# Summing the squares of four query columns in plain float32 instead of two rounded parts

## Chip, cores and metric

The kernel runs on one core of a Trainium2 chip (trn2). The metric is the device time of one execution in microseconds (us). The kernel before was timed three times: 1103.29, 1103.33 and 1104.15 us, median 1103.33.

## The reference

One encoder block of hidden width 2048 on 272 tokens (16 learned meta tokens and 256 tokens of a 4 x 64 grid), all in float32. In outline:

```python
hn = rmsnorm(h, mix_norm_g[l])
proj = hn @ w_in[l]
q_a = rmsnorm(q_a.reshape(B, L, NA_HEADS, NA_HEAD_DIM), na_q_g[l])      # group A: 8 heads of 128
k_a = rmsnorm(k_a.reshape(B, L, NA_HEADS, NA_HEAD_DIM), na_k_g[l])
out_a = neighbourhood_attention(q_a, k_a, v_a, na_rpb[l], na_meta_bias[l])
out_b = mla_attention(cq, ckv, k_pe, ...)                               # group B: 8 heads, q and k of 192
h = h + jnp.concatenate([rmsnorm(out_a, na_out_g[l]), rmsnorm(out_b, mla_out_g[l])], -1) @ w_out[l]
h = h + conv_glu(rmsnorm(h, ffn_norm_g[l]), w_gate[l], w_up[l], conv_w[l], conv_b[l], w_down[l])
return h[:, N_META:]
```

What matters here is the rmsnorm of the queries of every head: for each token and head the squares over the head's 128 (group A) or 192 (group B) dimensions are summed, and the queries' scores are scaled by the reciprocal root of their mean plus eps.

## The kernel before

Tokens lie along the free axis and features along the 128 partitions. Token order is reversed, so the 256 grid tokens come first, and then the meta tokens. The convolution at the end still reaches one meta token, so queries are computed for 258 columns (`NT`): two blocks of 128 columns and **two meta queries**, columns 256 and 257. Heads are worked on in four pairs (`na_pair`, `mla_pair`), each pair once for group A and once for group B; with two heads that makes four small query columns per pair and group, the "few meta queries" of the change.

Precision: nearly every matmul is done three times on values split in two parts. `hi` is the value rounded to the type F32R, `lo` the remainder (`split_plain`: ScalarE copies into `hi`, VectorE subtracts into `lo`), and hi x hi, hi x lo and lo x hi are added up in a PSUM bank. A matmul whose operands have the type F32 is a plain float32 matmul; `ones_sum` (line 931) issues one with the constant `ones`.

The 128 main query rows of each block get their sum of squares on ScalarE, from transposed queries with an accumulating Square. The four small query columns get it from a matmul: `na_queries` (line 1310) and `mla_queries` (line 1497) let ScalarE write the squares into a small tile `sq8` (4 columns for group A, 8 for group B, whose second four are the rotary part). Then `small_sums` (line 1248) runs, once per pair and group, eight times in all: VectorE copies the squares, rounded, into the first half of `sq8r` (line 1251); GpSimd subtracts to get the remainder in the second half (line 1252); and TensorE multiplies each part with the rounded ones (`ones_r`), two matmuls of 128 x 4 by 128 x 2 for group A, four for group B, 24 in all. The sums go into `v`, `rstd` (line 923: logarithm, exponential, one refinement) turns them into the scale `rq`, and the heads' score tiles `na_tile` and `mla_tile` start after that.

Keys have a function of their own, `keys` (line 1161), 16 calls: squares of 272 columns, split into `hi` and `lo`, two matmuls with `ones_r` on the left, then `rstd` and a scaled, split key.

The order of the work is not that of the source. Every helper is a Python generator that yields the engine and an estimated cost before it issues its instruction (`ACT` line 247, `TT` line 253, `COPY` line 265, `PTT` on GpSimd line 277, `MM` line 287 with the costs of `cost` in line 281). A planner, `Flow` (line 124), keeps a clock per engine and always issues the instruction that could start earliest; on a hop between engines it adds 700 ns on the way to TensorE, 200 ns away from it and 140 ns otherwise (line 129). Each engine then executes its own instructions in exactly that order, and semaphores hold an instruction back until its inputs are there. So the costs decide the order, and a planned time that is too early makes an engine stand still in front of an instruction, with all that is queued behind it. `fl.cur.t += x` inside a helper moves its next instruction x ns later in the plan.

Slots (`Slots`, line 109) are sets of buffers that helpers take and give back in planned order. The sums, the score tiles and the attention outputs share two PSUM banks, `sps` (line 316). TensorE's main thread is `attention_weights` (line 1798): it goes through the projections pair by pair, and its matmuls (`mm3`, lines 734 to 736: two with the weights' `hi`, one with the weights' `lo`) fill TensorE between those of the attention. Weights arrive through SyncE's DMA queue and are split by ScalarE (`whi`) and VectorE (`wlo`). After the four pairs come the output projection (group B's heads `ob`, then group A's `oa`) and the gated MLP, whose up and down projections partly use a scheme of seven products.

Of the kernel before, what the change touches and what calls it, by code (L numbers as in the profile page):

```python
# [9 lines left out]
F32 = mybir.dt.float32  # L10
F32R = mybir.dt.float32r
AF = mybir.ActivationFunctionType
ALU = mybir.AluOpType
AX = mybir.AxisListType

P = 128
D_MODEL = 2048
SEQ = 256
# [200 lines left out]
def encoder_block(ctx: ExitStack, tc: tile.TileContext, io):  # L219
    nc = tc.nc  # L220
    ctx.enter_context(tc.manual_schedule())
    fl = Flow()
# [6 lines left out]
    apool = actx.enter_context(tc.tile_pool(name="apool", bufs=1))  # L229

    def tiles(pool, n, shape, name, dt=F32):
        return [pool.tile(shape, dt, tag=f"{name}{i}", name=f"{name}{i}") for i in range(n)]


    def size(ap):
        n = 1
        for s in ap.shape[1:]:
            n *= s
        return n
# [25 lines left out]
    def COPY(out, a):  # L265
        yield "dve", 68 + 1.04 * size(out)
        nc.vector.tensor_copy(out, a)
# [9 lines left out]
    def PTT(out, a, b, op):  # L277
        yield "pool", 90 + (2.7 if fl.cur.t < 4e5 else 3.9) * size(out)
        nc.gpsimd.tensor_tensor(out, a, b, op)  # L279

    def cost(l, r):
        n, m = size(r), l.shape[-1]
        if r.dtype != F32R:
            return max(1.69 * n, 3.33 * m, 50)
        return 0.445 * n + 3 if n >= 256 else max(0.84 * n, 0.84 * m, 27)

    def MM(items):

        yield "pe", sum(cost(l, r) for _, l, r, _, _ in items)
        for o, l, r, start, stop in items:  # L290
            nc.tensor.matmul(o, l, r, start=start, stop=stop)  # L291
# [18 lines left out]
    def one(slots):  # L310
        (t,) = yield slots, 1
        return t
# [169 lines left out]
    for w, f in enumerate(QUADS):  # L482

        g, end = f // 2, (*QUADS, MID)[w + 1] // 2
# [4 lines left out]
        for i in range(KC // 2):  # L489
            r = RowPair(io["w_up_s"][w][i], i, PW // 4, "up")  # L490
# [45 lines left out]
    n = len(others) - BEHIND  # L536
# [216 lines left out]
    ones = const("ones")  # L753
# [21 lines left out]
    for g in range(0, FC // 2 if MID_SUMS else 0, MID_SUMS or 1):  # L775
        n = min(MID_SUMS, FC // 2 - g)
        t = dpool.tile([P, n, PW // 4], F32, name=f"early_m{g}")
        w = io["w_down_m"][g : g + n].rearrange("g p c -> p g c")
        q, ev = PW // 4, Event()
        early.append((t, w[:, :, :q], w[:, :, 2 * q : 3 * q], ev))  # L780
        early_mid += [(t[:, i], ev) for i in range(n)]
    for g in range(FC // 2):
        ev, q, w = Event(), PW // 2, io["w_down_s"][g]
        if g % THIRD:
            t = dpool.tile([P, q], F32, name=f"early{g}")
            early.append((t, w[:, q : 2 * q], w[:, 2 * q : 3 * q], ev))
        else:
            t = dpool.tile([P, PW], F32, name=f"early{g}")
# [78 lines left out]
    p = pieces[0]  # L867
# [98 lines left out]
    ones_r = apool.tile([P, P], F32R, name="ones_r")  # L966
# [162 lines left out]
    qss = tiles(apool, 2, [P, 5 * QS + 4], "qs", F32R)  # L1129

    sq8 = tiles(apool, 2, [P, 8], "sq8")
    sq8r = tiles(apool, 2, [P, 2, 8], "sq8r", F32R)
    for t in [t.bitcast(F32) for t in qss] + sq8:
        nc.gpsimd.memset(t, 0.0)
    qss, sq8 = Slots(qss), Slots(list(zip(sq8, sq8r)))
    q_raw = Slots(tiles(apool, 1, [P, 3, NT], "qraw"))
    cols = tiles(apool, 8, [P, 8], "cols")
    for t in cols:
# [8 lines left out]
    for h in range(HEADS):  # L1147
        t = apool.tile([P, 2, NT], F32R, name=f"ob{h}")
        ob.append((t[:, 0, :], t[:, 1, :]))
        t = apool.tile([P, 2, NT], F32R, name=f"oa{h}") if h < 6 else hl[KC - HEADS + h]  # L1150
# [10 lines left out]
    def keys(ps, k, gain, n_dims, extra, ev):  # L1161

        hi, lo = k[:, 0, :], k[:, 1, :]
        kg = yield from one(scr)
        yield from ACT(kg[:, :L], ps[:, :L], AF.Copy)
        fl.put(acc, ps)
        sq, a, r = yield scr, 3
        v = sq[:, :L]
        yield from ACT(hi, kg[:, :L], AF.Square)
        yield from ACT(v, kg[:, :L], AF.Square)  # L1170
        yield from TT(lo, v, hi.bitcast(F32), ALU.subtract)
        yield ev_ones
        ss = yield from one(sps)
        yield from MM([(ss[:, :L], ones_r, hi, True, False), (ss[:, :L], ones_r, lo, False, True)])
        yield ev
        yield from STT(v, ss[:, :L], 1.0 / n_dims, extra, ALU.mult, ALU.add)
        fl.put(sps, ss)
        yield from rstd(r[:, :L], v, a[:, :L])
        fl.put(scr, a)
        fl.put(scr, sq)  # L1180
        yield ev_gains
        yield from STT(kg[:, :L], kg[:, :L], gain, r[:, :L], ALU.mult, ALU.mult)
        yield from split_plain(hi, lo, kg[:, :L])
        fl.put(scr, kg)
        return r
# [61 lines left out]

    def small_sums(q8, n):

        f, r = q8  # L1250
        yield from COPY(r[:, 0, : 4 * n], f[:, : 4 * n])
        yield from PTT(
            r[:, 1, : 4 * n], f[:, : 4 * n], r[:, 0, : 4 * n].bitcast(F32), ALU.subtract
        )
        yield ev_ones
        ss = yield from one(sps)
        m = [(g, i) for g in range(n) for i in range(2)]
        yield from MM(
            [(ss[:4, 0:2], r[:, i, 4 * g : 4 * g + 4], ones_r[:, 0:2], (g, i) == m[0], (g, i) == m[-1])
             for g, i in m]  # L1260
        )
        fl.put(sq8, q8)
        return ss
# [46 lines left out]
    def na_queries(s, pss):  # L1310
        q = yield from one(q_raw)
        s.q = yield from one(na_q)
        for c, ps in enumerate(pss):
            yield from ACT(q[:, c, :], ps[:, :NT], AF.Copy)
            fl.put(acc, ps)
        for c in range(2):
            fl.spawn(split_query(s, c, q))
        s.qs = yield from one(qss)
        fl.spawn(small_queries(s))
        w = yield from one(cols)  # L1320
        q8 = yield from one(sq8)
        yield from ACT(
            q8[0][:, 0:4].rearrange("p (c t) -> p c t", c=2), q[:, 0:2, SEQ:], AF.Square
        )
        pt = yield from one(tps)
        yield from TR(
            [(pt[:, (2 * c + i) * P : (2 * c + i + 1) * P], q[:, c, i * P : (i + 1) * P])
             for c in range(2) for i in range(2)]
        )
        fl.spawn(free_raw(s, q))  # L1330
        for j in range(4):
            t = pt[:, j * P : (j + 1) * P]
            yield from ACT(t, t, AF.Square, accum_out=w[:, j : j + 1])
        fl.put(tps, pt)
        ss = yield from small_sums(q8, 1)
        v = yield from one(v6)
        yield ev_em1c
        yield from STT(v[:, 0:4], w[:, 0:4], 1.0 / HD, em1_c, ALU.mult, ALU.add)
        yield from STT(v[:4, 4:5], ss[:4, 0:1], 1.0 / HD, em1_s, ALU.mult, ALU.add)
        fl.put(sps, ss)  # L1340
        s.rq = yield from one(rq6)
        yield from rstd(s.rq, v, w[:, 0:6])
        fl.put(v6, v)
        fl.put(cols, w)
        fl.set(s.ev_q)
# [151 lines left out]
    def mla_queries(s, pss):  # L1497
        q = yield from one(q_raw)
        s.q = yield from one(mq)
        for c in range(3):  # L1500
            yield from ACT(q[:, c, :], pss[c][:, :NT], AF.Copy)
            if c < 2:
                fl.put(acc, pss[c])
                fl.spawn(split_query(s, c, q))
        g, t, tmp = yield scr, 3
        yield from ACT(g[:, :NT], pss[2][:, :NT], AF.Copy, scale=gains[:, 2:3])
        fl.put(acc, pss[2])
        s.qs = yield from one(qss)
        fl.spawn(small_queries(s))
        fl.spawn(mla_rope(s, g, t, tmp))  # L1510
        w = yield from one(cols)
        q8 = yield from one(sq8)
        f = q8[0].rearrange("p (g c t) -> p g c t", g=2, c=2)
        yield from ACT(f[:, 0], q[:, 0:2, SEQ:], AF.Square)
        for c in range(2):
            e = slice(64 * c, 64 * c + 64)
            yield from ACT(f[e, 1, c, :], q[e, 2, SEQ:], AF.Square)
        for i in range(2):
            pt = yield from one(tps)
            sl = slice(i * P, (i + 1) * P)  # L1520
            yield from TR(
                [(pt[:, :P], q[:, 0, sl]), (pt[:, P : 2 * P], q[:, 2, sl]),
                 (pt[:, 2 * P : 3 * P], q[:, 1, sl])]
            )
            if i:
                fl.spawn(free_raw(s, q))
            for c in range(2):
                t = pt[:, c * QK_DIM : (c + 1) * QK_DIM]
                yield from ACT(t, t, AF.Square, accum_out=w[:, 2 * c + i : 2 * c + i + 1])
            fl.put(tps, pt)  # L1530
        ss = yield from small_sums(q8, 2)
        v = yield from one(v6)
        yield ev_emc
        yield from STT(v[:, 0:4], w[:, 0:4], 1.0 / QK_DIM, emc_c, ALU.mult, ALU.add)
        yield from STT(v[:4, 4:5], ss[:4, 0:1], 1.0 / QK_DIM, emc_s, ALU.mult, ALU.add)
        fl.put(sps, ss)
        s.rq = yield from one(rq6)
        yield from rstd(s.rq, v, w[:, 0:6])
        fl.put(v6, v)
        fl.put(cols, w)  # L1540
        fl.set(s.ev_q)
# [938 lines left out]
```

## Time and profile before

| what | value |
|---|---|
| median of three runs | 1103.33 us |
| the profiled execution's own time | 1103.1 us |
| its span, first to last instruction | 1101.3 us |
| granted TensorE clock | 0.999 |
| TensorE matmuls, busy | 1094.4 us, 8164 records |
| VectorE, busy | 1015.2 us, 1922 instructions |
| ScalarE, busy | 753.8 us, 1514 instructions |
| GpSimd, busy | 147.6 us, 217 instructions |
| DMA | 262.73 MB, mean 239 GB/s |

Times in the trace count from the first instruction. A matmul's record lasts from its start to the modelled arrival of its last result, so neighbouring matmuls overlap in the records and the distance from start to start tells how long TensorE was taken. Names of tiles stand without their numbers: `sq8` is printed as `sq`, `sq8r` as `sq8r`, the PSUM banks as `bank`.

### The profile page before, as it was taken

How to read it: one execution, taken by the hardware profiler on the slowest of the kernel's cores; microseconds unless marked ns; L12 is line 12 of the kernel's file. 1: busy time of each engine (PE TensorE's matmuls, PEld its weight loads, DVE VectorE, ACT ScalarE, POOL GpSimd, SP SyncE). 2: the span in 40 equal slices, each digit the busy share in tenths (PEclk: the TensorE clock that was granted, in tenths of full speed). 3: DMA queues.
4: the chain of work that ended last, by engine and by line, in shares of the span. 5: the costliest groups of instructions: out<-in, count | busy, mean ns of one | idle time of the engine just before them, and what ended most of it. 6: DMA issues, size and time to landing. Idle time of an engine off the chain costs nothing. (4 is left out here: it accounts for less than half of the span.)

```text
span 1101.3 us, 22419 instructions
## 1 busy us (share of the span) xinstructions
PE 1094.4 (99%) x8164; PEld 1046.1 (95%) x8164; DVE 1015.2 (92%) x1922; ACT 753.8 (68%) x1514; POOL 147.6 (13%) x217
## 2 busy tenths in 40 slices
PE   9999999999999999999999999999999999999998
PEld 9999999999999999999999999999999999888887
DVE  8969888888878989999999999999999989999997
ACT  8788979788646776666666666665665656666663
POOL 3211222323433400000000000000000000301041
PEclk9999999999999999999999999999999999999999
DMA  8775678577877778665766667767888879699891
GB/s 322 252 236 168 196 224 238 156 200 182 263 202 214 234 245 326 209 200 189 237 216 206 217 202 240 249 199 274 271 307 289 285 236 328 206 315 330 291 342 44
DMA packets 81752, 262.73 MB, mean 239 GB/s; under 512 B 9225, under 2 KB 12937, under 8 KB 81641
## 3 DMA queue, kind: packets, MB, share of 16 engines
q1 hardware_dynamic: 77880, 251.46, 67.4%
q0 software_dynamic: 3472, 9.57, 5.4%
q8 instruction: 64, 1.05, 0.4%
q14 instruction: 48, 0.39, 0.1%
q10 hardware_dynamic: 288, 0.27, 0.1%
HBM read 243.82 MB, written 34.08 MB: 252 GB/s over the span
## 5 line engine op out<-in xcount | busy, mean ns | idle before, releaser
L251 ACT ACTIVATE whi<-raw 128x512 fp32r<-128x512 f32 (+2 forms) x493 | 353.1, 736 | 159.4 <-PE bank L735 53.7
L255 DVE TENSOR_TENSOR wlo<-raw,whi 128x512 fp32r<-128x512 f32 (+2 forms) x493 | 407.4, 847 | 30.6 <-ACT whi L251 29.7
L734 PE MATMUL bank<-hl,whi 128*128 128x258 f32 (+1 forms) x1208 | 347.8, 288 | 0.1
L735 PE MATMUL bank<-hl,whi 128*128 128x258 f32 (+1 forms) x1208 | 343.6, 284 | 0.0
L736 PE MATMUL bank<-hl,wlo 128*128 128x258 f32 (+1 forms) x1208 | 343.2, 284 | 0.3 <-DVE wlo L255 0.3
L736 PEld LDWEIGHTS bank<-hl,wlo 128*128 128x128 f32 x1208 | 229.7, 190 | 0.8 <-DVE wlo L255 0.6
L735 PEld LDWEIGHTS bank<-hl,whi 128*128 128x128 f32 x1208 | 229.3, 190 | 0.1
L734 PEld LDWEIGHTS bank<-hl,whi 128*128 128x128 f32 x1208 | 228.2, 189 | 0.8 <-ACT scr L251 0.3
L291 PE MATMUL bank<-whi,act 128*128 128x256 f32 (+1 forms) x574 | 143.5, 302 | 0.0
L2064 PE MATMUL bank<-hl,whi 128*128 128x512 f32 x384 | 136.6, 395 | 0.0
L2065 PE MATMUL bank<-hl,wlo 128*128 128x256 f32 x384 | 107.7, 280 | 0.0
L291 PEld LDWEIGHTS bank<-whi,act 128*128 128x128 f32 x574 | 100.2, 189 | 5.1
L251 ACT ACTIVATE whi<-more_raw 128x1024 fp32r<-128x1024 f32 (+1 forms) x72 | 74.1, 1029 | 39.8 <-DVE more_raw L255 22.7
L279 POOL TENSOR_TENSOR mt<-mt 128x256 f32<-128x256 f32 x3 | 12.2, 4083 | 653.0 <-ACT mt L251 653.0
L255 DVE TENSOR_TENSOR wlo<-more_raw,whi 128x1024 fp32r<-128x1024 f32 (+1 forms) x72 | 85.6, 1189 | 3.2 <-ACT whi L251 3.1
L291 PE MATMUL bank<-wlo,act 128*128 128x256 f32 (+1 forms) x287 | 86.8, 302 | 0.0
L2064 PEld LDWEIGHTS bank<-hl,whi 128*128 128x128 f32 x384 | 72.1, 188 | 14.9
L2065 PEld LDWEIGHTS bank<-hl,wlo 128*128 128x128 f32 x384 | 72.4, 188 | 0.0
L291 PE MATMUL bank<-whi,sin 128*128 128x256 f32 (+1 forms) x250 | 70.0, 325 | 0.0
L251 ACT ACTIVATE whi<-halves 128x1024 fp32r<-128x1024 f32 (+2 forms) x54 | 50.6, 955 | 20.9 <-PE bank L291 8.2
L255 DVE TENSOR_TENSOR wlo<-halves,whi 128x1024 fp32r<-128x1024 f32 (+2 forms) x54 | 59.2, 1122 | 0.5 <-ACT whi L251 0.3
L291 PEld LDWEIGHTS bank<-wlo,act 128*128 128x128 f32 x287 | 54.3, 189 | 2.2
(325 smaller groups left out, 2231.2 us busy)
## 6 DMA issues: line engine op xcount, KB each, us to landing
raw<-in_w_gate SPq DMA_DIRECT2D x88, 512.0 KB, 5.2
raw<-in_w_in SPq DMA_DIRECT2D x52, 512.0 KB, 4.8
raw<-in_w_up SPq DMA_DIRECT2D x48, 512.0 KB, 4.5
raw<-in_w_up_s SPq DMA_DIRECT2D x40, 512.0 KB, 4.5
raw<-in_w_out SPq DMA_DIRECT2D x32, 512.0 KB, 5.7
sin<-s_down SPq DMA_DIRECT2D x28, 512.0 KB, 6.7
raw<-in_w_down_m SPq DMA_DIRECT2D x21, 512.0 KB, 5.8
s_down<-sums SPq DMA_DIRECT2D x20, 512.0 KB, 6.9
```

Source lines behind the costliest of these rows:

```text
L251: nc.scalar.activation(out, in_, f, **kw)
L255: nc.vector.tensor_tensor(out, a, b, op)
L279: nc.gpsimd.tensor_tensor(out, a, b, op)
L291: nc.tensor.matmul(o, l, r, start=start, stop=stop)
L734: nc.tensor.matmul(ps, whi, xhi, start=start, stop=False)
L735: nc.tensor.matmul(ps, whi, xlo, start=False, stop=False)
L736: nc.tensor.matmul(ps, wlo, xhi, start=False, stop=stop)
L2064: nc.tensor.matmul(ps, whi, x, start=start, stop=False)
L2065: nc.tensor.matmul(ps[:, :n], wlo, x[:, 0, :], start=False, stop=stop)
```

## The change

`small_sums` no longer makes two parts. The tile `sq8r`, the copy on VectorE and the subtraction on GpSimd are gone, and one plain float32 matmul with `ones` takes the place of two rounded ones with `ones_r`: one for group A, two for group B, 12 in all. Beside this, both `small_sums` and `keys` add 250 ns to the planned time of their thread just before their matmul, after they have taken a bank.

```diff
     sq8 = tiles(apool, 2, [P, 8], "sq8")
-    sq8r = tiles(apool, 2, [P, 2, 8], "sq8r", F32R)
     for t in [t.bitcast(F32) for t in qss] + sq8:
         nc.gpsimd.memset(t, 0.0)
-    qss, sq8 = Slots(qss), Slots(list(zip(sq8, sq8r)))
+    qss, sq8 = Slots(qss), Slots(sq8)
...
         yield ev_ones
         ss = yield from one(sps)
+        fl.cur.t += 250.0
         yield from MM([(ss[:, :L], ones_r, hi, True, False), (ss[:, :L], ones_r, lo, False, True)])
...
     def small_sums(q8, n):
 
-        f, r = q8
-        yield from COPY(r[:, 0, : 4 * n], f[:, : 4 * n])
-        yield from PTT(
-            r[:, 1, : 4 * n], f[:, : 4 * n], r[:, 0, : 4 * n].bitcast(F32), ALU.subtract
-        )
         yield ev_ones
         ss = yield from one(sps)
-        m = [(g, i) for g in range(n) for i in range(2)]
+        fl.cur.t += 250.0
         yield from MM(
-            [(ss[:4, 0:2], r[:, i, 4 * g : 4 * g + 4], ones_r[:, 0:2], (g, i) == m[0], (g, i) == m[-1])
-             for g, i in m]
+            [(ss[:4, 0:2], q8[:, 4 * g : 4 * g + 4], ones[:, 0:2], g == 0, g == n - 1)
+             for g in range(n)]
         )
```

In `na_queries` and `mla_queries` only `q8[0]` becomes `q8`, since the slot now holds one tile.

More of the change, by code (lines that the diff above doesn't have):

```diff
@@ L1322, in na_queries @@
         yield from ACT(
-            q8[0][:, 0:4].rearrange("p (c t) -> p c t", c=2), q[:, 0:2, SEQ:], AF.Square
+            q8[:, 0:4].rearrange("p (c t) -> p c t", c=2), q[:, 0:2, SEQ:], AF.Square
         )
@@ L1512, in mla_queries @@
         q8 = yield from one(sq8)
-        f = q8[0].rearrange("p (g c t) -> p g c t", g=2, c=2)
+        f = q8.rearrange("p (g c t) -> p g c t", g=2, c=2)
         yield from ACT(f[:, 0], q[:, 0:2, SEQ:], AF.Square)
```

## Prediction

> **What bounds the kernel now.** I read the page first, then the busy time by stages, then what TensorE waited for, and only then single stretches of the timeline around the instructions that the change touches.
>
> ```profile
> span 1101.3 us, 22419 instructions
> PE 1094.4 (99%) x8164; PEld 1046.1 (95%) x8164; DVE 1015.2 (92%) x1922; ACT 753.8 (68%) x1514; POOL 147.6 (13%) x217
> PEclk9999999999999999999999999999999999999999
> ```
>
> TensorE (PE) is busy 1094.4 of 1101.3 us at a full clock, so the program is one long stream of matmuls. A few us could be won by taking away waits; anything more would need fewer or shorter matmuls. The stages say where the waits are:
>
> ```profile
> 60.00:300.00 240.00, 239.04 (x1973) 235.90 (x1972) 209.90 (x556) 204.83 (x637) 66.31 (x122) 1.00 0.71 205
> 300.00:960.00 660.00, 660.00 (x5064) 638.67 (x5064) 621.74 (x1116) 418.87 (x680) 43.97 (x44) 1.00 0.73 240
> 960.00:1000.00 40.00, 39.53 (x180) 31.89 (x179) 39.83 (x45) 26.83 (x31) 4.59 (x4) 1.00 0.95 332
> ```
>
> The columns after the window are its length and the busy time of PE, weight loads, VectorE (DVE), ScalarE (ACT) and GpSimd (POOL). All that the change edits lies between 60 and 300 us, the attention stage, and there PE is idle for 0.96 us in all. From 300 to 960 it is never idle. Near the end, between 960 and 1000, VectorE (39.83 of 40 us) and the DMA (0.95) are full, and PE loses 0.47 us. The waits of PE over the whole program confirm how little there is:
>
> ```profile
> PE bank L291 <- DVE wlo L255: 0.5, 1, 0.5
> PE bank L291 <- POOL sq8r L279: 0.5, 2, 0.3
> PE bank L291 <- ACT whi L251: 0.4, 1, 0.4
> PE bank L736 <- DVE wlo L255: 0.3, 1, 0.3
> PE bank L291 <- ACT p L251: 0.2, 1, 0.2
> ```
>
> The row of `sq8r` belongs to this change: that tile is the one removed. Ends of matmuls are modelled here, so a visible idle time understates a wait by as much as the matmul before it seems to reach into it. From here on I use distances from start to start.
>
> **The change part by part.** Eight calls of small_sums lose a cast on VectorE, a subtraction on GpSimd and the two-part small matmuls:
>
> ```profile
> L291 PE MATMUL bank<-ones_r,sq8r x24: 164/165/169, 66.1 to 252.9; 128*4 128x2 f32 x24
> L267 DVE CAST sq8r<-sq x8: 150/158/721, 65.3 to 251.9; 128x4 fp32r<-128x4 f32 x4, 128x8 fp32r<-128x8 f32 x4
> L279 POOL TENSOR_TENSOR sq8r<-sq,sq8r x8: 201/322/697, 65.5 to 252.1; 128x4 fp32r<-128x4 f32 x4, 128x8 fp32r<-128x8 f32 x4
> ```
>
> *Cast and subtraction as work.* Eight casts at the median of 158 ns are 1.3 us of VectorE, eight subtractions at 322 ns are 2.6 us of GpSimd. VectorE is busy 209.90 of 240 us in this stage and GpSimd 66.31, both beside a full PE, so I cost their going at zero. The cover is the projection matmuls. They matter only through PE's wait for their result, which is the next term.
>
> *The wait.* PE stands still in front of a small matmul at these places:
>
> ```profile
> 75.27 0.17 PE L291 MATMUL bank<-ones_r,sq8r 128*4 128x2 f32 x1
> 75.73 0.22 PE L291 MATMUL bank<-ones_r,sq8r 128*4 128x2 f32 x3 [0.29 <-POOL sq8r L279]
> 75.81 0.37 PE L734 MATMUL bank<-hl,whi 128*128 128x272 f32 x1
> 76.02 0.29 PE L735 MATMUL bank<-hl,whi 128*128 128x272 f32 x1
> ```
>
> ```profile
> 124.33 0.17 PE L291 MATMUL bank<-ones_r,sq8r 128*4 128x2 f32 x1
> 124.66 0.22 PE L291 MATMUL bank<-ones_r,sq8r 128*4 128x2 f32 x3 [0.17 <-POOL sq8r L279]
> ```
>
> ```profile
> 252.25 0.41 PE L291 MATMUL bank<-mkp,mqr 128*128 128x272 f32 x2
> 252.84 0.19 PE L291 MATMUL bank<-ones_r,sq8r 128*4 128x2 f32 x2 [0.18 <-ACT p L251]
> ```
>
> Three small matmuls in 0.22 us, one of them lasting 0.165, start 0.055 / 2 = 0.027 us apart: that is the step where nothing is waited for. The first matmul (the cast's half) started at 75.27, the second (the subtraction's half) at 75.73, so the wait is 0.46 - 0.03 = 0.43 us. At 124.33 it is 0.33 - 0.03 = 0.30. The third case is another one. The second of the two matmuls before it starts about 0.12 us after 252.25, so the small one is late by 252.84 - 252.37 - 0.13 = 0.34 us; but there two releasers came almost together:
>
> ```profile
> 252.10 0.64 POOL L279 TENSOR_TENSOR sq8r<-sq,sq8r 128x4 fp32r<-128x4 f32 x1 [1.58 <-DVE cols L255]
> 252.12 0.58 ACT L251 ACTIVATE p<-bank,cols,rq 128x272 f32<-128x272 f32 x1 [0.40 <-DVE cols L255]
> ```
>
> GpSimd ended at 252.74 and ScalarE, which had still to read the score bank that the sum wants, at 252.70. Without the subtraction the bank is late next, and only 0.04 us goes. Sum of this term: 0.43 + 0.30 + 0.04 = 0.77 us won.
>
> The new matmul waits for the squares themselves, and those are old by then:
>
> ```profile
> L251 ACT ACTIVATE sq<-qraw x16: 192/207/246, 60.5 to 247.3; 128x4 f32<-128x4 f32 x8, 64x2 f32<-64x2 f32 x8
> ```
>
> First square at 60.5, first small matmul at 66.1; last at 247.3 against 252.8. Over 5 us of lead at both ends, so no new wait on ScalarE.
>
> *The small matmuls in plain float32.* "Half as many" holds in the code: 24 become 12. In the trace one plain float32 matmul leaves two records. Line 981 issues one such matmul, for `sqx`:
>
> ```profile
> 36.86 0.62 PE L291 MATMUL bank<-sqx,consts 128*128 128x272 f32 x2
> 37.12 0.49 PE L734 MATMUL bank<-hl,whi 128*128 128x272 f32 x1
> 37.45 0.29 PE L735 MATMUL bank<-hl,whi 128*128 128x272 f32 x1
> ```
>
> ```profile
> L291 PE MATMUL bank<-sqx,consts 128*128 128x272 f32 x2 | 0.6, 392 | 0.0
> ```
>
> ```profile
> 265.26 0.41 PE L291 MATMUL bank<-nak,ones_r 128*128 128x272 f32 x2
> 265.51 0.29 PE L734 MATMUL bank<-hl,whi 128*128 128x272 f32 x1
> ```
>
> The middle row gives the mean of one record, 392 ns. The two records start 0.62 - 0.39 = 0.23 us apart, while the rounded type of the same width takes (265.51 - 265.26) / 2 = 0.125 each. So I expect 12 x 2 = 24 records again. With two columns the stream hardly counts. Lower bound: a record per matmul after all, 12 x 0.027 = 0.32 us won. Upper bound: each of the 24 records takes twice its step, 0.65 us lost. I take zero, since the nearest row, the present 128x2 record, sits at a step that its two columns don't explain (136 times as many columns take only 4.6 times as long). The price around a group stays: after 75.81 the next matmul comes 0.21 us later instead of 0.125, with either type.
>
> The Trainium skill, "FP8 and Floating Point Precision", section "TensorE Precision Notes", says that true float32 makes four passes through the array; two records of 0.23 us against one of 0.125 agree with four. By that alone, passes would double from 24 to 48, an estimate of the upper bound above. The skill's "TensorE: Matmul & The Clock Gate", section "Back-to-back issue gap", gives matmuls of 1 to 64 columns the same floor of some 25 ns; the step of 0.027 here agrees, and by it two passes of two columns fit in one step, giving the zero.
>
> *The 250 ns of the planner.* The order of instructions on every engine is written by the planner. Before, a small sum was booked at least 140 + 72 + 140 + about 100 ns after the last square (two hops, cast, subtraction, by its costs in lines 129, 266 and 278), then 700 for the way to PE; now 250 and then 700, so it stands about 200 ns earlier in PE's order than before, 1.6 matmuls. The sixteen key sums move 250 ns later, two matmuls. Behind a key sum on PE stand the projection's matmuls; they gain where the sum was early:
>
> ```profile
> 89.31 0.29 PE L736 MATMUL bank<-hl,wlo 128*128 128x272 f32 x1
> 89.70 0.53 PE L291 MATMUL bank<-nak,ones_r 128*128 128x272 f32 x2
> ```
>
> Here the sum came 0.39 - 0.126 = 0.26 us late, and two matmuls ahead of it would cover that: 0.26 won. Against it stands a reordered stage, in which other instructions meet their inputs a little later. Bounds: 0.26 won, or one or two new waits of the size seen above (0.3 to 0.4 us each), 0.8 lost. I take zero. What follows a key sum has slack: the last MLA head must be ready for the output projection,
>
> ```profile
> L734 PE MATMUL bank<-ob,whi x128: 280/283/367, 280.8 to 330.4; 128*128 128x258 f32 x128
> L263 DVE SCALAR_TENSOR_TENSOR ob<-bank,vecs,ob x8: 465/478/486, 107.7 to 276.7; 128x258 fp32r<-128x258 f32 x8
> ```
>
> and it is written at 276.7 + 0.5 = 277.2, while its turn (after 7 heads x 2 tiles x 3 matmuls x 0.12 = 5 us) comes at 285.8: 8.6 us.
>
> **The sum.** The profiled execution took 1103.1 us, 1.8 around its span of 1101.3; the median of the three runs is 1103.33, 0.2 above it. 1103.1 - 0.77 = 1102.3, and on the scale of the median 1102.5.
>
> **The rivals.**
>
> *It is lost at the end.* At 999 us PE waits for VectorE:
>
> ```profile
> 998.01 1.59 DVE wlo L255
> 999.60 0.04 issue
> 999.64 1.43 PE bank L291 x5
> ```
>
> The chain that ended last runs back from here through VectorE and DMA to 978. If VectorE and the DMA don't move with PE, PE only waits 0.77 us longer there, and the time stays at 1103.3. For it: both are full in 960 to 1000. Against it: before that their inputs and free buffers come from a stage in which PE never waits, so they move with PE.
>
> *Float32 is dear.* Every record doubled: 0.65 lost of 0.77 won, 1103.2.
>
> *All waits of the stage go.* Beside the terms above, the rest of the third one (0.30) and the key sum's (0.26) vanish, and the tail wait of 0.47 with them: 0.77 + 0.30 + 0.26 + 0.47 = 1.80, thus 1101.5. Nothing in the profile says that the new order finds all of them.
>
> *Slower: the two score banks.* The sums, the scores and the attention outputs share two banks (`sps`). The planner takes the bank before it adds the 250 ns, so 24 times a bank is booked longer, and every later taker is pushed. If the real order then meets banks that are still being read, as at 252.84, each costs PE some 0.34 us. Ten such places of the 24 give 3.4 - 0.77 = 2.6 us more, 1106.0; it decides from the third place on, where the loss passes the gain. For it: that wait is already there once. Against it: once in 24 sums, and PE has projections to fill with.
>
> **Chances.** Forecast (1102.1 to 1103.0) 0.47; lost at the end 0.20; float32 dear 0.10; all waits go 0.09, of which 0.05 by over 0.2%, should other waits of the stage go with them; slower 0.14, of which 0.11 by over 0.2%. A change of 0.2%, 2.2 us, is about what a measurement of this kernel tells from none. So faster 0.05, within 0.2% 0.84, slower 0.11. The range goes from 1101.3, all waits gone and the 0.2 between profile and median, up to 1104.9, seven places of the slower case (7 x 0.34 - 0.77 = 1.6); it leaves out the worse half of that case and the best of the other side.
>
> **What would show it.** No instruction on `sq8r`; 24 float32 records of 128x2 on `sq` about 0.027 us apart; no GpSimd wait in front of a small sum; PE's idle time between 60 and 300 us down from 0.96 to some 0.5. The forecast is wrong if new waits of ScalarE or VectorE appear before PE in that stage, or if the stage ends earlier and the wait at 999 us has grown by as much.

## The result and the profile after

The kernel after takes **1104.74 us** (median of 18 runs) against 1103.33 before (18 runs): ratio 1.0014, 95% interval 1.0008 to 1.0021. It is slower by 1.4 us, less than 0.2%, where 0.8 us faster was forecast. Its profiled execution took 1104.62 us with a span of 1102.8.

First the page of the kernel after, its second and third line as before:

```profile
span 1102.8 us, 22391 instructions
PE 1096.4 (99%) x8164; PEld 1046.8 (95%) x8164; DVE 1018.1 (92%) x1914; ACT 755.2 (68%) x1514; POOL 142.2 (13%) x209
```

Eight instructions fewer on VectorE, eight fewer on GpSimd, and still 8164 matmul records: half the small matmuls in the code are no fewer records. The tile's own rows say the same, and that nobody waits for the squares any more (the list of waiters is empty):

```profile
L291 PE MATMUL bank<-consts,sq x24: 164/164/168, 65.5 to 254.7; 128*4 128x2 f32 x24
L251 ACT ACTIVATE sq<-qraw x16: 200/207/262, 59.8 to 249.5; 128x4 f32<-128x4 f32 x8, 64x2 f32<-64x2 f32 x8
```

The busy times of the attention stage, with the columns as in the prediction:

```profile
60.00:300.00 240.00, 239.02 (x1955) 233.86 (x1954) 210.59 (x545) 203.80 (x630) 60.16 (x113) 1.00 0.71 204
```

Between 60 and 300 us PE shows the same busy time as before, 239.02 against 239.04, but it started 1955 matmuls there instead of 1973. A busy share near 100% hides this, because the modelled ends of the records reach over the gaps. So I measure the attention stage by position: from the first record of line 734 that reads `late` to the last that reads `ob`. These are the same two matmuls of the weight stream in every kernel here. The first of the two rows comes from the tile `late`, the second from `ob`; the times after the durations are the starts of the first and the last record. First the missing row of before, then both of after:

```profile
L734 PE MATMUL bank<-late,whi x64: 277/287/480, 59.4 to 229.9; 128*128 128x258 f32 x48, 128*128 128x272 f32 x16
```

```profile
L734 PE MATMUL bank<-late,whi x64: 278/288/480, 58.7 to 230.9; 128*128 128x258 f32 x48, 128*128 128x272 f32 x16
L734 PE MATMUL bank<-ob,whi x128: 279/283/370, 282.3 to 331.9; 128*128 128x258 f32 x128
```

Before, the stage took 330.4 - 59.4 = **271.0 us**; after, 331.9 - 58.7 = **273.2**. All of the loss, and 0.7 us more, lies here. The 0.7 comes from the first 59 us, in which both kernels run the same instructions in the same order; over the kernels of this study that starting point lay between 58.2 and 59.9, so it is a spread of single executions. Behind the stage nothing changes: at the last `ob` matmul after stands 1.5 us later than before, and its span is 1.5 us longer.

The waits of PE in the kernel after, between 60 and 300 us:

```profile
PE bank L291 <- ACT p L251: 0.4, 2, 0.2
PE bank L297 <- POOL p L279: 0.3, 1, 0.3
PE bank L291 <- DVE mkp L255: 0.2, 1, 0.2
```

The two waits for `sq8r` are gone, and so is the one at 252.84, where the sum met a bank that ScalarE was still reading (`ACT p`). Four others stand in their place; two of them are again for `ACT p`. Taken from start to start they are larger than this view shows:

```profile
84.48 0.29 PE L736 MATMUL bank<-hl,wlo 128*128 128x272 f32 x1
85.01 0.52 PE L291 MATMUL bank<-nak,ones_r 128*128 128x272 f32 x2 [0.24 <-ACT p L251]
...
134.01 0.38 PE L297 MATMUL bank<-ident,p 128*128 128x128 f32 x2
134.72 0.33 PE L297 MATMUL bank<-ident,p 128*128 128x128 f32 x1 [0.33 <-POOL p L279]
...
193.37 0.54 PE L291 MATMUL bank<-late,mq 128*128 128x272 f32 x3
194.09 0.39 PE L291 MATMUL bank<-mkp,mqr 128*128 128x272 f32 x1 [0.18 <-DVE mkp L255]
...
253.02 0.29 PE L736 MATMUL bank<-hl,wlo 128*128 128x272 f32 x1
253.49 0.39 PE L291 MATMUL bank<-late,mq 128*128 128x272 f32 x1 [0.18 <-ACT p L251]
```

A record of 272 columns takes a step of 0.126 us, a transpose 0.11. The four waits are 0.53 - 0.13 = 0.40; 134.72 - 134.12 - 0.11 = 0.49 (the second transpose of the pair starts 0.38 - 0.27 after 134.01); 194.09 - 193.62 - 0.13 = 0.34 (the third of the three at 193.37 + 0.54 - 0.29); and 0.47 - 0.13 = 0.34. Together 1.57 us: a key sum, a transposed probability and two score tiles came before their inputs. Not all of it is new. In before a key sum was 0.26 us late (89.70, in the prediction), and so was a transposed probability, though the list of its waits names neither:

```profile
134.57 0.80 PE L297 MATMUL bank<-ident,p 128*128 128x128 f32 x3
135.12 0.62 PE L291 MATMUL bank<-late,mq 128*128 128x272 f32 x3
```

Three transposes at 0.11 make 0.33; the next matmul came after 0.55, so 0.22 was lost. About 1.1 us of the 1.57 are new, and a list of waits that is empty doesn't mean that PE never stood.

The plain float32 matmuls have a price too. The same place in both kernels, before first:

```profile
65.99 0.29 PE L736 MATMUL bank<-late,wlo 128*128 128x272 f32 x1
66.12 0.19 PE L291 MATMUL bank<-ones_r,sq8r 128*4 128x2 f32 x2
66.17 0.37 PE L734 MATMUL bank<-hl,whi 128*128 128x272 f32 x1
66.38 0.29 PE L735 MATMUL bank<-hl,whi 128*128 128x272 f32 x1
```

```profile
65.31 0.29 PE L736 MATMUL bank<-late,wlo 128*128 128x272 f32 x1
65.53 0.19 PE L291 MATMUL bank<-consts,sq 128*4 128x2 f32 x2
65.65 0.39 PE L734 MATMUL bank<-hl,whi 128*128 128x272 f32 x1
65.88 0.29 PE L735 MATMUL bank<-hl,whi 128*128 128x272 f32 x1
```

From the projection matmul ahead of the sum to the second one behind it: 0.39 us before, 0.57 after. Two projection steps belong to it anyhow (0.25), so a sum costs 0.14 us in two rounded parts and **0.32 in plain float32**. The two small records stay 0.03 us apart; the extra lies around them, 0.09 ahead of the first (0.22 instead of 0.13), 0.07 from the first small record to the next large one (0.12 instead of 0.05) and 0.02 behind that. Eight sums make 8 x 0.18 = 1.4 us.

At the three places of the prediction 1.07 us of waits are won (0.43 + 0.30 + 0.34). So 1.4 of price and 1.1 of new waits less 1.07 make 1.4 of the 2.2 us by which the stage grew. The rest lies in shorter delays that were not traced to places.

Two theories came out of this comparison. **A:** the loss is the price of plain float32. **B:** it is the changed order of the instructions. Both start from the 1.07 us of waits won.

### The profile page after: what moved, and what is told of

Same layout as the page of the kernel before. It is cut to its first block, busy times and chain, and to the rows that moved or that the text cites. A ratio compares the mean times of both kernels' runs of the same rounds, so it can differ in the third digit from the quotient of the medians.

```text
span 1102.8 us, 22391 instructions
## 1 busy us (share of the span) xinstructions
PE 1096.4 (99%) x8164; PEld 1046.8 (95%) x8164; DVE 1018.1 (92%) x1914; ACT 755.2 (68%) x1514; POOL 142.2 (13%) x209
## 4 chain that ended last, share of the span: by engine, by line
PE 89%; DVE 4%; ACT 3%; DMA 2%; issue 1%; SPq 0%; POOL 0%; DVEq 0%; ACTq 0%; POOLq 0%
PE bank L291 26%; PE bank L734 15%; PE bank L735 15%; PE bank L736 15%; PE bank L2059 11%; PE bank L2060 6%; PE bank L297 2%; DVE wlo L255 2%; ACT whi L251 1%; ACT scr L251 1%; DMA raw<-in_w_cq 1%; DVE scr L263 1%; DMA early<-in_w_down_s 1%; DMA scr<-scr 0%; ACT qraw L251 0%
```

## The experiments

The kernels were timed in three groups, each with before beside them on one chip. Before had a median of 1103.03 us in the first group, 1103.08 in the second and 1103.17 in the third; each other kernel has 5 to 11 executions. "Stage" is the distance defined above, 271.0 before and 273.2 after; it comes from one profiled execution of each kernel.

### Float32 with every other instruction where it was

```diff
     def small_sums(q8, n):
+        yield "dve", 68 + 1.04 * 4 * n
+        yield "pool", 90 + (2.7 if fl.cur.t < 4e5 else 3.9) * 4 * n
         yield ev_ones
         ss = yield from one(sps)
-        fl.cur.t += 250.0
...
+        yield "pe", 27 * 2 * n
+        for g in range(n):
+            nc.tensor.matmul(ss[:4, 0:2], q8[:, 4 * g : 4 * g + 4], ones[:, 0:2], start=g == 0, stop=g == n - 1)
```

The planner is charged for work that is not issued, and no 250 ns are added, neither here nor for the keys.

> Cast and subtraction gone, plain float32 matmuls, but the planner is still charged for the old cast, subtraction and matmuls and gets no 250 ns, so that every other instruction stands where it stood before. Theory A (plain float32 has a price of its own on PE, about 0.18 us for each of the 8 sums, read from the profile after): the sums cost 2.6 us of PE instead of 1.3 without waits and 2.4 with them, so about +0.2 us against before, 1103.5. Theory B (float32 is free, the loss is all in the new order): the waits of 1.1 us go and nothing comes, 1102.2.

Measured: 1102.82 us, ratio 1.0002 (0.9993 to 1.0011). In the trace of this run:

```profile
L734 PE MATMUL bank<-late,whi x64: 278/288/480, 58.8 to 229.6; 128*128 128x258 f32 x48, 128*128 128x272 f32 x16
L734 PE MATMUL bank<-ob,whi x128: 277/283/367, 280.5 to 330.1; 128*128 128x258 f32 x128
```

The stage is 330.1 - 58.8 = 271.3. The list of PE's waits between 60 and 300 us is empty. Apart from the sums, the records of every engine stand in the same order as in before. So all that the title of the change names, with nothing else moved, costs 0.3 us of the stage and nothing that the timing can tell from zero. That fits 1.4 us of price against 1.07 us of waits. Both theories had half of it. A is right that the price is there, B that it does not make the result.

### Rounded sums in the old and in the new order

```diff
-    sq8 = tiles(apool, 2, [P, 8], "sq8")
+    sq8 = tiles(apool, 2, [P, 8], "sq8", F32R)
...
-            [(ss[:4, 0:2], q8[:, 4 * g : 4 * g + 4], ones[:, 0:2], g == 0, g == n - 1)
+            [(ss[:4, 0:2], q8[:, 4 * g : 4 * g + 4], ones_r[:, 0:2], g == 0, g == n - 1)
```

In one kernel the planner keeps the costs of before, in the other those of after, so that each order stays as it was; the traces bear this out on every engine.

> As the kernel with float32 in the old order, but ScalarE writes the squares rounded, and 12 rounded matmuls sum them: the remainder of the squares is left out of the sum. Both theories: the waits for GpSimd (1.1 us) and 12 steps of 0.027 us (0.3) go, 1101.9. Theory A says it is 1.7 us faster than its float32 sister, theory B 0.3.

> The kernel after with its order untouched, but the squares rounded and summed by 12 rounded matmuls: the remainder of the squares is left out of the sum. Theory A: the 8 sums fall from 2.6 us to 1.0, so 1.6 us less than after, 1103.1. Theory B: the order is unchanged, so 1104.4 (0.3 less for twelve records).

Measured: 1102.30 us, ratio 0.9993 (0.9984 to 1.0002) in the old order; 1104.89, ratio 1.0016 (1.0007 to 1.0024) in the new one. Stages: 328.8 - 58.5 = 270.3 and 331.7 - 58.8 = 272.9. In the new order the place of the first sum now reads:

```profile
65.45 0.29 PE L736 MATMUL bank<-late,wlo 128*128 128x272 f32 x1
65.58 0.17 PE L1255 MATMUL bank<-ones_r,sq 128*4 128x2 f32 x1
65.60 0.37 PE L734 MATMUL bank<-hl,whi 128*128 128x272 f32 x1
65.81 0.29 PE L735 MATMUL bank<-hl,whi 128*128 128x272 f32 x1
```

The sum costs 0.36 - 0.25 = 0.11 us, a third of 0.32. Yet the stage fell by only 0.3 us against after, and the time did not fall at all. New waits took much of the rest, as the same kernel's list shows:

```profile
PE bank L291 <- ACT p L251: 0.4, 2, 0.2
PE bank L297 <- POOL p L279: 0.3, 1, 0.3
PE bank L297 <- ACT qraw L251: 0.2, 1, 0.2
PE bank L291 <- DVE mkp L255: 0.2, 1, 0.2
PE bank L734 <- ACT scr L251: 0.2, 1, 0.2
PE bank L291 <- DVE late L255: 0.2, 1, 0.2
```

Three rows are as in the kernel after; the others are places that PE reached later before. Theory A, which wanted 1103.1, is out as the cause of the result. B is left: at the same sums, the new order costs 272.9 - 270.3 = 2.6 us of the stage with rounded sums and 273.2 - 271.3 = 1.9 with float32.

### Without the two delays

```diff
-        fl.cur.t += 250.0
```

in `keys` and in `small_sums` of the kernel after.

> The kernel after without the two lines that add 250 ns in the plan, in the sums and in the keys. If the 250 ns made the new waits in front of key sums, scores and transposes (about 1.9 us in the profile after against 0.9 before), those go back, 1103.5 to 1103.8. If it is the removed planning steps that reorder the stage, it stays at 1104.7 or gets worse, since the small sums then stand even earlier.

Measured: 1106.04 us, ratio 1.0025 (1.0015 to 1.0036); stage 333.2 - 58.9 = 274.3. So the 250 ns do not make the new waits: without them it is worse by 1.1 us of the stage. The removed planning steps reorder the stage, and in this one order the delays take a part of that back.

Two sub-theories of B followed. O1: an early sum starts the heads too early, so its planned time decides. O2: the order of before is a good one among many, and nearly any change of the plan costs something.

### The sum booked where it was, and later

```diff
-        fl.cur.t += 250.0
+        fl.cur.t += 453.0 if n == 1 else 470.0
```

without the delay in `keys`; and the same with `900.0`.

> The kernel after, but the small sum is booked 453 ns (group A) or 470 ns (group B) after the last square instead of 250, which is where the old cast and subtraction put it; no 250 ns for the keys. Only the planned time on VectorE and GpSimd is given free against the run with float32 in the old order (1102.8 us, 3.2 us of PE time above the plain stream between 55 and 385 us). Theory O1 (the heads of a pair start too early when the sum is booked early, and their scores then bunch up in front of PE): with the sum back at its old time the stage goes back, 1102.8 and about 3.2 us. Theory O2 (the old order happens to be a good one, any change of the plan costs one to three us): 1104 to 1106, 4.5 to 6 us.

> As the run before it in this list, with 900 ns instead of 453 or 470. O1: as good or better than with the old time, 1102.5 to 1102.9, since the heads start later still and there is slack behind them. O2: 1104 to 1106.

Measured: 1106.99 us, ratio 1.0033 (1.0021 to 1.0046), and 1108.01, ratio 1.0044 (1.0032 to 1.0057); stages 276.1 and 275.7. The sum is booked as long after its squares as before, or longer, and the loss is larger than after. O1, my own favourite, falls as a matter of planned time. In PE's real order the sums did not go all the way back: the third one has 518 larger matmuls of the stage ahead of it in before, 491 in after, 500 and 503 here.

The first of these stages holds something else as well. In the run with 453 and 470 ns the granted clock falls to half from 110.2 to 113.6 us, right behind two waits of PE (1.15 us ahead of 109.01 and 0.50 ahead of 110.06). The run with 900 has two waits of the same length and keeps the full clock. One microsecond of each, the run with 453 and 470 first; the clock is the third number from the end:

```profile
111.00:112.00 1.00, 1.00 (x6) 1.00 (x6) 0.11 (x1) 0.00 (x0) 0.06 (x1) 0.50 0.70 139
111.00:112.00 1.00, 1.00 (x11) 1.00 (x10) 0.42 (x1) 0.39 (x2) 0.58 (x3) 1.00 1.08 236
```

PE starts 6 matmuls in it instead of 11. From the 3.4 us at half the clock I estimate 1.7 us, which leaves about 274.4 of the 276.1 for the order. The one execution of this kernel with a mean clock of 1.0 took 1105.69 us, still more than after.

### The delay of the keys alone, and of the sums alone

The first kernel is before with the one added line in `keys`; the second is after without it.

> The kernel before with one edit, the 250 ns in front of the key sums; the small sums keep their two rounded parts. O1: the small sums stay where they were and the heads' keys come a little later, so within 0.5 us of before, 1102.5 to 1103.5. O2: 1 to 3 us more than before, 1104 to 1106.

> The kernel after with the 250 ns in front of the small sums alone, none for the keys. If the 250 ns act as a shift with a sense (a sum or a key that stands later meets its input), the time lies between the kernel after (1104.7) and the one with neither (1106.0). O2: it is one more order among many, anywhere from 1104 to 1108.

Measured: 1105.90 us, ratio 1.0024 (1.0014 to 1.0034), stage 274.4; and 1106.42, ratio 1.0030 (1.0020 to 1.0041), stage 276.2. This last stage again holds 3.4 us at half the clock (from 111.3 us), and its profiled execution took 1108.00 us, 1.6 above the median. The delays have no sense of their own. With float32 sums, none gives 1106.0, that of the sums alone 1106.4, both 1104.7; on before, that of the keys alone costs 2.8 us.

### A change of the plan that is aimed at nothing

```diff
-    TO_PE, FROM_PE, OTHER = 700.0, 200.0, 140.0
+    TO_PE, FROM_PE, OTHER = 700.0, 200.0, 145.0
```

in the kernel with float32 in the old order; and `135.0` in the untouched kernel before.

> Float32 sums with the old costs, as in the run in the old order, but the planner books every hop between two engines other than TensorE at 145 ns instead of 140: a change of the order that is aimed at nothing. O1: the sums keep their place within 15 ns, so within 0.5 us of the run in the old order, 1102.3 to 1103.3. O2: 1104 to 1106.

> The kernel before, untouched but for the planner, which books a hop between two engines other than TensorE at 135 ns instead of 140. Theory O2 (the order that before has is a good one among many, and any other costs one to five us in the attention stage): 1104 to 1108, and 5 to 8 us above the plain stream between 55 and 385 us against 2.9 before. Theory O3 (only plans in which the sums or the keys were moved, or hops lengthened, are bad): within 0.5 us of before, 1102.6 to 1103.6.

Measured: 1107.43 us, ratio 1.0040 (1.0027 to 1.0052), stage 275.9; and 1106.86, ratio 1.0031 (1.0019 to 1.0042), stage 274.0. Five nanoseconds in the planner's books, and nothing else, cost more than the whole change. This is before with 135:

```profile
L734 PE MATMUL bank<-late,whi x64: 277/287/480, 58.8 to 230.2; 128*128 128x258 f32 x48, 128*128 128x272 f32 x16
L734 PE MATMUL bank<-ob,whi x128: 280/283/367, 282.7 to 332.8; 128*128 128x258 f32 x128
```

and its waits between 60 and 300 us:

```profile
PE bank L291 <- ACT p L251: 1.0, 2, 0.5
PE bank L291 <- POOL sq8r L279: 0.8, 4, 0.3
PE bank L297 <- POOL p L279: 0.2, 1, 0.2
```

The wait for `sq8r`, two times in before, now comes four times, and two score banks are late. O2 stands; O3, by which only a moved sum or key or a longer hop makes a bad plan, falls. Of eight orders other than the old one (after's among them), all eight are slower, with stages of 272.9 to 276.2 us against 270.3 to 271.5 in all kernels that keep the old order; after's is the best of the eight. Three of the eight are near copies of each other: compared record by record, the sums booked as before and later differ from the delay of the sums alone in about 35 and 93 of PE's 8164 records, and all three have the same longest wait (`ACT pt`, 1.1 us). So these are about six separate orders.

### Taking the old waits away in the old order

Here the two rounded parts stay whole, and the planner's books are those of before. First the subtraction is issued on VectorE in the place of GpSimd's:

```diff
-        yield from PTT(
-            r[:, 1, : 4 * n], f[:, : 4 * n], r[:, 0, : 4 * n].bitcast(F32), ALU.subtract
-        )
+        yield "pool", 90 + (2.7 if fl.cur.t < 4e5 else 3.9) * 4 * n
+        nc.vector.tensor_tensor(
+            r[:, 1, : 4 * n], f[:, : 4 * n], r[:, 0, : 4 * n].bitcast(F32), ALU.subtract
+        )
```

then the matmuls are issued only right ahead of the instruction that reads the sum:

```diff
-        yield from MM([(ss[:4, 0:2], r[:, i, 4 * g : 4 * g + 4], ones_r[:, 0:2], ...) for g, i in m])
+        yield "pe", 27 * 2 * n
+        held.append((ss, r, m))
...
+        issue_held()
         yield from STT(v[:4, 4:5], ss[:4, 0:1], 1.0 / HD, em1_s, ALU.mult, ALU.add)
```

> The kernel before in its own order, two rounded parts kept in full, with the subtraction on VectorE in the place where GpSimd had it. The waits of PE for GpSimd (0.43 + 0.30, and 0.04 of the third) shrink to what the cast leaves, some 0.1 each: 0.5 us less than before, 1102.5. The price of plain float32 doesn't arise: the sums cost 1.3 us and what is left of the waits.

> As the run with the subtraction on VectorE, and the planner's books are untouched, but the small matmuls are written into PE's order one to three projection matmul groups later, right ahead of the instruction that reads the sum. All three waits of before (1.07 us) go if no other instruction waits for the sum: 1101.9 to 1102.2, which would be under both kernels. If the reader on VectorE is now late and holds up weights behind it, no gain.

Measured: 1103.03 us, ratio 0.9999 (0.9990 to 1.0008), stage 330.9 - 59.9 = 271.0; and 1103.07, ratio 1.0000 (0.9991 to 1.0009), stage 330.3 - 58.8 = 271.5. The first misses its forecast of a shorter wait; PE waits for VectorE instead of GpSimd for as long:

```profile
PE bank L291 <- DVE sq8r L1253: 0.5, 2, 0.3
```

The second does what it should at the sums. Its list of waits between 60 and 300 us has one row left, and that row names another place:

```profile
PE bank L297 <- POOL p L279: 0.3, 1, 0.3
```

The stage is no shorter all the same. The 1.07 us came back elsewhere, part of it in this wait, which from start to start is 0.5 us here and was 0.2 in before. So neither version is proved faster than before.

## Why the prediction was wrong, point by point

- **What bounds the kernel, and where it can change:** right. PE's stream sets the end, all of the difference arises between 59 and 332 us, and it goes through to the end unaltered.
- **Cast and subtraction cost nothing as work:** right; the old order without them keeps the stage within 0.3 us of before.
- **The wait, 0.77 us won:** the waits went, and more than that, for with float32 in the old order the third went too (1.07 us). As a gain it held only with the rounded type, by 0.7 us of the stage in place of 1.1 and 0.3 for fewer records.
- **Float32 at zero, at most 0.65 lost:** wrong in size. The step of 0.03 us between the records was right, and 24 records too. The price sits around the group and measured 0.18 us a sum, 1.4 us. The bound was drawn from steps inside the group alone; "The price around a group stays", with either type, is the sentence that failed. Four passes against one floor, the two rules of the Trainium skill that I weighed ("FP8 and Floating Point Precision", section "TensorE Precision Notes"; "TensorE: Matmul & The Clock Gate", section "Back-to-back issue gap"), both speak of the inside of the group; there the trace agrees with the floor.
- **The 250 ns and the new order at zero, between 0.26 won and 0.8 lost:** this is the step that decided. The order cost 1.9 us of the stage with float32. I read the shift of each instruction and its slack one by one, found slack everywhere, and took that for safety. The shift itself was mis-sized: it was put at 1.6 matmuls, but counted by the larger matmuls ahead of them in the stage, the eight sums stand from 27 places earlier (518 to 491) to 11 later (1075 to 1086). The runs show that changed orders cost 1.9 to 4.6 us of the stage here against the old order with the same kind of sums, whatever the edit (4.8 and 4.9 in the two profiles with a stretch at half the clock). The sign that the prediction named for its being wrong, new waits of PE for ScalarE or VectorE in this stage, is what came (`ACT p`, `DVE mkp`).
- **Lost at the end:** refuted. The delay at the last `ob` matmul, 1.5 us, is also that of the span, and a gain goes through as well: with rounded sums in the old order that matmul starts 1.6 us earlier than in before (328.8), and the span is 1.5 us shorter (1099.8).
- **All waits of the stage go:** no. With float32 in the old order those at the sums went, but a key sum (at 89.00) and a transposed probability are still late by 0.27 us each.
- **Slower, by the two score banks:** the right sign for a reason too narrow. A bank that is still being read is one of the late inputs (`ACT p` in the lists), beside transposes, keys and rotary keys; and its trigger, longer booking by the 250 ns, is refuted, since without them it is worse. It is luck that 1104.74 lies under the upper end of the range, 1104.9, and within the 0.2%: that end was worked out from seven late score banks and free float32 sums, while the runs show the order and the price of float32.

Shown: the share of the order and the share of float32, each with the other held. Only argued: why the old order is good; that its costs were fitted to it is likely but no run shows it. Open: why single waits that are taken away come back elsewhere. That PE then runs into the next late input fits these cases, but the rows show it only for a part of the time: in the rounded kernel in the new order, and at the transposed probability behind the late sums.

## What to carry to other kernels

Where a planner writes the order of all engines, an edit to one small step is two edits: its own cost, and a new order for everything behind it. Price the second by runs with a neutral change of the plan before believing the first, and test an edit with the plan's books held as they were. When the stage's engine is full, a wait that is removed may count only up to the next late input; and a busy share of 99.6% can hide two us, so compare positions of the same matmul.

## What the runs showed of the hardware that was not expected

A plain float32 matmul with four weight columns breaks the stream of rounded ones around it. Its weight load starts together with it, while the rounded one's started ahead of the matmul (66.00 against 66.12). The weight loads of the kernel after and then of before, at the same place:

```profile
65.19 0.19 PEld L736 LDWEIGHTS bank<-late,wlo 128*128 128x128 f32 x1
65.53 0.09 PEld L291 LDWEIGHTS bank<-consts,sq 128*4 128x4 f32 x2 [0.15 <-issue]
65.65 0.19 PEld L734 LDWEIGHTS bank<-hl,whi 128*128 128x128 f32 x1
```

```profile
65.87 0.19 PEld L736 LDWEIGHTS bank<-late,wlo 128*128 128x128 f32 x1
66.00 0.21 PEld L291 LDWEIGHTS bank<-ones_r,sq8r 128*4 128x4 f32 x2
66.15 0.19 PEld L734 LDWEIGHTS bank<-hl,whi 128*128 128x128 f32 x1
```

In the kernel after the weight loads stand idle for 0.15 us ahead of the float32 group. A plain float32 matmul of 272 columns with 128 weight columns, at 36.86 us in before, began 0.13 us after the matmul ahead of it and so showed no such gap. Whether the four columns or the short stream make the difference was not tried.
